# A two-layer encoder trunk: ScalarE and VectorE work behind later weight casts, PSUM banks by hand, operands loaded during P7

## The chip, the cores and the metric

The kernel runs on one core of one Trainium2 chip. The metric is the device time of one execution in microseconds (us), median of the runs shown. TensorE (PE) multiplies, VectorE (DVE) and ScalarE (ACT) work on elements, GpSimd (POOL) does a little of that and starts DMAs, and SyncE (SP) starts nearly all loads. Each engine works through its own instructions in the order in which they stand.

## What is computed

The reference runs two layers over 512 tokens of width 2048:

```
h = rmsnorm(x, g_pre)
z = h @ w_in                       # gq gk gv gg ga | aq ak av ag
log_a = log_sigmoid(ga @ w_alpha + b_alpha) / 16
o_gla = rmsnorm(gla_chunk_causal(gq, gk, gv, log_a), g_gla) * silu(gg)
o_att = rmsnorm(chunk_band_attention(aq, ak, av, rel_bias), g_att) * silu(ag)
y = concatenate([o_gla, o_att]) @ w_out
return x + rmsnorm(y, g_post)
```

The input projection has 14 column blocks of 512, the output projection four. The first blocks to be computed are the gates (AG, GG) and the attention values (AV).

## The kernel before

**A pair of blocks as seven products.** Two column blocks are computed together by `Pair` (L383). The matrix product is cut into halves of rows, of the inner dimension and of columns, and computed with seven products, P1 to P7, where eight would be plain. Each product runs over four chunks c = 0 to 3; one chunk of one product is a *job*, 12 matmuls of 128x512 in the front pairs (L480). A product's left operand is a block of activations or a sum of such blocks (S1 for P5, S2 for P6, S4 for P3, S3 for P7, and A22 for P4; P1 and P2 use plain blocks a11c and a12c). Its right operand is a weight block or a sum of weight blocks: `H` holds the running sum, `raw` a freshly loaded block. Numbers are kept in two parts to hold float32 precision: `wh` is the rounded weight, cast by ScalarE (L235), and `wl` the rest, subtracted by VectorE (L240). Weight sums for P5, P6 and P4 are made by VectorE at L224. So a job needs, in this order: a DMA from `in_w_dram` (L170, on SP's queue), perhaps a weight sum (L224), a cast on ScalarE (1.05 us), a subtraction on VectorE (1.22 us), then its matmuls.

**What is prepared ahead.** All jobs stand in one list, `stream`. After the matmuls of each job, `ahead` (L281) issues the load for up to five jobs on, the cast for up to four on and the low part for up to three on. There are four buffers each of `raw`, `H`, `wh` and of the operands `sa`, and three of `wl`. Program order on each engine is thus the order in which the Python code issues, as far as the scheduler, which works with its own cost model, does not move an instruction ahead; `tc.issue_after(x)` makes an instruction stand behind x.

**The front pairs.** Each layer begins with three pairs, (AG0, AG1), (GG0, GG1) and (AV0, AV1). A *head* runs P1 and P2 of the three in the order P1 of the first, P1 of the second, P2 of the first, P2 of the second, P1 of the third, P2 of the third (`HEAD`). Meanwhile the activations are scaled and split: in layer 0, `prep_chunk` scales a chunk (L690 on ScalarE, L688 on VectorE), casts it (L113) and subtracts (L114), which gives the operand a11c or a12c in use a little later. Then the rest of each pair runs in turn: P5, a mix of P6 and P3, P7, P4. The second and third pair ("second" in the code) load H again at P5, and with it the S1 operand from DRAM (L214, into the slots g8, g11, g14 and g15), where the first pair takes its S1 from SBUF.

**The banks.** The sums stand in PSUM: two banks X and two banks Y of the pool `ps_mm`, which has four in rotation. X takes P1 and P2, then P6, P7; Y takes P5 and P3. ScalarE copies p1 (L408) and later puts it back as X's first value (L415, in `open`); after P7 it copies X to Y (L503), on which P4 adds. P4's result in Y leaves through silu on ScalarE (L834) for the gates, or through a scaled copy (L944) for the values. The banks of the next pair are handed out in rotation, so that P5 of the next pair fills the two banks that P4 of the pair before has just filled.

**Side steps.** Scaling of activations, token squares (L535), sums, norms and the forget gate are Python generators in a list `tasks`; `pump` runs the next step of the first one some times after each job. They are issued in between, on the same engines. At the end of the second front pair, ScalarE loads another table of functions (L61), and VectorE scales the forget gate's input (L872).

Of the kernel before, what the change touches and what calls it, by code (L numbers as in the profile page):

```python
# [35 lines left out]
def hybrid_trunk(  # L36
# [19 lines left out]
    ps_mm = ctx.enter_context(tc.tile_pool(name="ps_mm", bufs=4, space=PSUM))  # L56
# [104 lines left out]
    lows = []  # L161
    rows = {}

    class Job:
# [8 lines left out]
        def load(self):  # L173
# [42 lines left out]
        def high(self):  # L216
# [17 lines left out]
            with tc.issue_after(last_evac[0]) if last_evac[0] else nullcontext():  # L234
                last_cast[0] = nc.scalar.copy(self.wh, src).ins  # L235

# [11 lines left out]
    stream = []  # L248
    for l in range(L):
        infos = [{"early": True, "direct": True}, {"early": True, "second": True}, {"early": True, "second": True}]  # L250
        for k, i in HEAD:
# [12 lines left out]
    done = {"load": 0, "high": 0, "low": 0}  # L264
# [7 lines left out]
    def take(l, blk, kind, c):  # L272
# [3 lines left out]
        for what in ("load", "high", "low"):  # L276
            prepare(what, i + 1)
# [62 lines left out]
    def std_gemm(l, blk, outs, chunks, operand, evac, rate=0.0, skip=0, lag=0, strict=False):  # L340
        pss = {o: ps_mm.tile([P, W], F32, tag="mm", name=nm("mm")) for o in outs}
# [35 lines left out]
    def pair_banks():  # L377
        return [ps_mm.tile([P, W], F32, tag="mm", name=nm("mm")) for _ in range(2)]
# [4 lines left out]
    class Pair:  # L383
        def __init__(self, l, pair, consume, feature_major=False, early=False, end=False, scaled=True, seeded=False, keep=ev):
# [3 lines left out]
            self.banks = {"X": pair_banks, "Y": pair_banks, "Z": aux_banks}  # L388
# [22 lines left out]
        def open(self, *names):  # L411
            for name in names:
                self.acc[name] = self.banks[name]()
            for t in range(2):
                nc.scalar.copy(self.acc["X"][t], self.keep["p1"][t])  # L415
# [71 lines left out]
        def run(self, prods, rate=0.0, skip=0, after=None):  # L487
            pace = Pace(rate, skip)
            for k, c in prods:
# [3 lines left out]
                if c == self.last:  # L493
                    if k == "P1":
                        self.copies("p1", self.acc["X"])
                    elif k == "P5":
                        self.copies("p5", self.acc["Y"])
                    elif k == "P6":
                        self.copies("x", self.acc["X"])
                    else:  # L500
                        if k == "P7" and self.seeded:
                            for t in range(2):
                                nc.scalar.copy(self.acc["Y"][t], self.acc["X"][t])  # L503
                        for t in range(2):
                            self.finished(k, t)
                        if k == "P7" and self.early and not self.seeded:
                            self.copies("x", self.acc["X"])
                if after is not None:
                    after(k, c)
                pace()  # L510

# [315 lines left out]
    def layer(l):  # L827
# [113 lines left out]
        def av_consume(j, h, t, src, comb):  # L941
# [16 lines left out]
            Pair(l, FRONT[1], gate_consume(0), scaled=False, **how),  # L958
            Pair(l, FRONT[2], av_consume, keep=early_kept, **how),
        ]  # L960
        for n, (k, i) in enumerate(HEAD):
# [5 lines left out]
        front[0].open("Y", "X")  # L967
        front[0].run(early_rest(C_IN), rate=1.0)
        drain()
        tasks.append(forget_gate())  # L970
        front[1].open("X", "Y")
        front[1].run(early_rest(C_IN), rate=0.25)
# [5 lines left out]
        front[2].open("Y", "X")  # L978
        front[2].run(early_rest(C_IN))
        S_on.clear()  # L980
# [175 lines left out]
        fast_gemm(l, PAIRS[0], qk_consume(0), rate=2.1, feature_major=True, scaled=False)  # L1156
        fast_gemm(l, PAIRS[1], qk_consume(1), rate=2.1, feature_major=True, scaled=False)
# [37 lines left out]
        fast_gemm(l, PAIRS[2], kq_consume, rate=2.1)  # L1195
# [171 lines left out]
        fast_gemm(l, PAIRS[3], gv_consume, rate=4, after=fetch_operands)  # L1367
# [93 lines left out]
        fast_gemm(l, W23, w_consume, rate=1.5, end=True, after=fetch_last, scaled=False)  # L1461
# [13 lines left out]
        std_gemm(l, NB_IN + 1, (2, 3), OO, operand_out, last_evac, rate=1.5, lag=3 if last else 2, strict=last)  # L1475
# [63 lines left out]
```

## Time and profile before

| quantity | value |
| --- | --- |
| runs | 1633.35, 1633.65 and 1630.3 us |
| median | 1633.35 us |
| the profiled execution's own time | 1632.18 us |
| its span in the profile | 1630.4 us |
| its mean granted TensorE clock | 0.992 |
| TensorE busy | 1602.3 us, 8818 matmuls |
| VectorE busy | 1258.3 us |
| ScalarE busy | 923.8 us |
| DMA, mean | 287 GB/s |

How to read the profile: times in rows are us from the start of the span. A row of the timeline has the start, the duration, the engine, the line of the kernel, the operation, what it writes and reads, and in square brackets how long the engine stood idle before it and what released it. "PEclk" is the clock that TensorE was granted, as a share of the full one. DMA share is the mean busy share of the core's 16 DMA engines. A busy TensorE may be at half its pace, so the count of matmuls in a stretch tells more than its busy time.

### The profile page before, as it was taken

To read this page: it belongs to the slowest core of one execution; us is meant where nothing else is said; L and a number is where in the kernel's file an instruction comes from. 1 tells how busy PE (TensorE), PEld (TensorE's weight loads), DVE (VectorE), ACT (ScalarE), POOL (GpSimd) and SP (SyncE) were. 2 spreads that over 40 slices of the span, in tenths; PEclk is the share of its full clock that TensorE was granted. 3 is DMA by queue.
4 is the path that set the end of the run, shared out by engine and by line. 5 is a ranking of instruction groups with operands and counts; after the bars stand their busy time and mean duration, and the time that the engine had idled before them with its cause. 6 is when DMAs were issued, how large, how long until landed. Compare 5 with 4: busy or idle time off the path is not lost.

```text
span 1630.4 us, 24529 instructions
## 1 busy us (share of the span) xinstructions
PE 1602.3 (98%) x8818; PEld 1359.0 (83%) x8818; DVE 1258.3 (77%) x1580; ACT 923.8 (57%) x1534; POOL 177.4 (11%) x302
## 2 busy tenths in 40 slices
PE   9999999999999999999999999999999999999997
PEld 6777879999988887788787877899999888777886
DVE  6778788786877866678878877877868778766887
ACT  8465554456676545554685545444566865445543
POOL 1121000000101001310121100000011011013100
PEclk9999999999999999999999999999999999999999
DMA  9959777867868689799968788678588686978986
GB/s 371 375 195 401 269 253 258 295 222 250 297 223 292 223 317 324 277 364 329 344 235 328 261 329 300 229 250 313 176 292 302 213 285 222 357 251 327 383 314 233
DMA packets 150618, 467.84 MB, mean 287 GB/s; under 512 B 16492, under 2 KB 35956, under 8 KB 150496
## 3 DMA queue, kind: packets, MB, share of 16 engines
q1 hardware_dynamic: 127232, 385.79, 67.0%
q0 software_dynamic: 22688, 79.53, 12.8%
q8 instruction: 70, 1.15, 0.3%
q10 hardware_dynamic: 576, 0.95, 0.2%
q14 instruction: 52, 0.43, 0.1%
HBM read 393.01 MB, written 72.11 MB: 285 GB/s over the span
## 4 chain that ended last, share of the span: by engine, by line
PE 89%; DMA 5%; DVE 2%; ACT 2%; issue 1%; SPq 0%; DVEq 0%; POOLq 0%; ACTq 0%
PE mm L480 49%; PE mm L467 20%; PE mm L360 10%; DMA raw<-in_w_dram 2%; PE ax L1051 2%; DMA H<-in_w_dram 2%; DVE wl L240 1%; PE ax L480 1%; PE ax L1034 1%; PE ax L1251 1%; PE ax L1217 1%; ACT wh L235 1%; PE ax L1013 1%; PE ax L1014 1%; DMA t<-r 1%
## 5 line engine op out<-in xcount | busy, mean ns | idle before, releaser
L240 DVE TENSOR_TENSOR wl<-raw,wh 128x1024 fp32r<-128x1024 f32 x256 | 312.0, 1221 | 123.3 <-PE mm L480 35.9
L235 ACT CAST wh<-raw 128x1024 fp32r<-128x1024 f32 x256 | 269.0, 1052 | 229.5 <-PE mm L480 96.1
L235 ACT CAST wh<-H 128x1024 fp32r<-128x1024 f32 x239 | 250.9, 1052 | 227.3 <-PE mm L480 90.6
L240 DVE TENSOR_TENSOR wl<-H,wh 128x1024 fp32r<-128x1024 f32 (+1 forms) x241 | 292.6, 1216 | 102.1 <-PE mm L480 46.3
L480 PE MATMUL mm<-wh,sa 128*128 128x512 f32 x1088 | 345.2, 392 | 0.0
L480 PE MATMUL mm<-wh,g 128*128 128x512 f32 x832 | 266.3, 399 | 9.3 <-ACT wh L235 6.0
L480 PEld LDWEIGHTS mm<-wh,sa 128*128 128x128 f32 x1088 | 203.2, 188 | 43.0 <-issue 1.5
L467 PE MATMUL mm<-sa,wh 128*128 128x256 f32 x1280 | 236.3, 285 | 0.0
L480 PE MATMUL mm<-wh,a 128*128 128x512 f32 x704 | 229.6, 397 | 2.1 <-ACT a L113 1.0
L480 PE MATMUL mm<-wl,sa 128*128 128x512 f32 x544 | 212.7, 391 | 0.0
L224 DVE TENSOR_TENSOR H<-H,raw 128x1024 f32<-128x1024 f32 x160 | 194.2, 1220 | 22.4 <-DMA H<-in_w_dram 14.3
L467 PEld LDWEIGHTS mm<-sa,wh 128*128 128x128 f32 x1280 | 199.4, 191 | 0.2
L480 PEld LDWEIGHTS mm<-wh,g 128*128 128x128 f32 x832 | 159.9, 193 | 46.3 <-ACT wh L235 8.3
L467 PE MATMUL mm<-sa,wl 128*128 128x256 f32 x640 | 180.7, 283 | 0.0
L480 PE MATMUL mm<-wl,g 128*128 128x512 f32 x416 | 165.9, 399 | 3.8 <-DVE wl L240 3.7
L480 PEld LDWEIGHTS mm<-wh,a 128*128 128x128 f32 x704 | 131.7, 188 | 35.4 <-issue 3.7
L480 PE MATMUL mm<-wl,a 128*128 128x512 f32 x352 | 138.4, 395 | 1.3 <-DVE wl L240 1.3
L467 PEld LDWEIGHTS mm<-sa,wl 128*128 128x128 f32 x640 | 122.3, 191 | 0.2
L480 PEld LDWEIGHTS mm<-wl,sa 128*128 128x128 f32 x544 | 102.2, 188 | 21.8 <-DVE wl L240 0.8
L480 PEld LDWEIGHTS mm<-wl,g 128*128 128x128 f32 x416 | 80.2, 193 | 23.3 <-DVE wl L240 6.4
L467 PE MATMUL mm<-a,wh 128*128 128x256 f32 x512 | 94.3, 285 | 0.0
L523 POOL TENSOR_TENSOR sm<-sm,cst 128x4 f32<-128x4 f32 (+2 forms) x40 | 49.3, 1233 | 325.3 <-DVE sm L1411 134.2
(208 smaller groups left out, 2269.9 us busy)
## 6 DMA issues: line engine op xcount, KB each, us to landing
raw<-in_w_dram SPq DMA_DIRECT2D x352, 512.0 KB, 5.5
sa<-S SPq DMA_DIRECT2D x128, 512.0 KB, 4.8
H<-in_w_dram SPq DMA_DIRECT2D x63, 512.0 KB, 5.7
S<-g POOLq DMA_DIRECT2D x32, 512.0 KB, 6.2
g<-S SPq DMA_DIRECT2D x32, 512.0 KB, 6.6
sa<-A SPq DMA_DIRECT2D x32, 512.0 KB, 6.0
oS<-g POOLq DMA_DIRECT2D x32, 512.0 KB, 6.4
sa<-oS SPq DMA_DIRECT2D x32, 512.0 KB, 5.1
```

The costliest lines, as they stand in the source:

```text
L224: nc.vector.tensor_tensor(out=h, in0=h, in1=r, op=ALU.add)
L235: last_cast[0] = nc.scalar.copy(self.wh, src).ins
L240: last_low[0] = nc.vector.tensor_tensor(out=self.wl[:, kk, :], in0=self.src[:, kk, :], in1=self.wh[:, kk, :].bitcast(F32), op=ALU.subtract ...
L360: mm = nc.tensor.matmul(pss[o], a[:, part, t], rhs[:, kk, :], start=(i == 0 and kk == 0 and m == 0), stop=(i == n - 1 and kk == 1 and m == 2),
L467: nc.tensor.matmul(dst, lhs[:, kk, f], a[:, part, tok], start=(fresh and kk == 0 and m == 0 and ft % 2 == 0), stop=(c == self.last and kk ...
L480: nc.tensor.matmul(out_ps[t], a[:, part, tok], rhs[:, kk, :], start=(fresh and kk == 0 and m == 0), stop=(c == self.last and kk == 1 and m ...
L523: return nc.gpsimd.tensor_tensor(out=out_r, in0=v, in1=mhalf[:, : v.shape[-1]], op=ALU.pow).ins
L1013: nc.tensor.matmul(ps[:, :n], self.qh[:, t], self.kl[:, :n], start=False, stop=False)
L1014: nc.tensor.matmul(ps[:, :n], self.ql[:, t], self.kh[:, :n], start=False, stop=True)
L1034: nc.tensor.transpose(ps[:, j * P : (j + 1) * P], self.prob[i][:, j * P : (j + 1) * P], ident)
L1051: nc.tensor.matmul(o, self.pt[i][:, j * P : (j + 1) * P], av[hd // 4, j // 2][:, j % 2, (hd % 4) * P : (hd % 4 + 1) * P], start=(j == 0), ...
L1217: mm = nc.tensor.matmul(self.ps_u[cc][:, tt * 256 : (tt + 1) * 256], kd[p][r, tt, hk], self.gv[p][r, tt, hv], start=True, stop=True,).ins
```

## The change

Four things are changed, all in the front pairs but the second and a part of the third.

1. `behind()` is new. While the front pairs run, the evictions at a product's end (now in `close`), the first values of X in `open`, and every side step that `pump` issues stand behind the last but one cast on ScalarE and the last but one low part on VectorE that have been issued.
2. `ps_mm` has one buffer for each of four tags, and `bank(i)` names them. Each pair says where its X lies (`x_bank` 0 or 2); Y lies in the two other banks. The front pairs have X in 0, 2, 0, so that P5 of the next pair fills the banks that P7 of the pair before leaves.
3. The operand loads (S1 to S4, A22) are taken out of `load` into `bring`, which `ahead` calls for four jobs ahead where `load` did it for five; `bring_next` loads the next front pair's S1 of chunk c behind the job P7 c of the pair that runs.
4. In layer 0 the norms of the second token half take turns with the token sums, where they stood ahead of them.

```
     @contextmanager
     def behind():
         if in_front[0] and len(casts) > 1 and len(lows) > 1:
             with tc.issue_after(casts[-2]), tc.issue_after(lows[-2]):
                 yield
         else:
             yield
...
+        def bring(self):
+            k, c, p = self.kind, self.c, self.pair
+            end = self.b0 == W23[0]
             name = LEFT.get(k)
+            if self.a is not None:
+                return
...
-        for what, n in (("load", 3), ("high", 3), ("low", 3), ("load", 4), ("high", 4), ("load", 5)):
-            if what != "load" and all(z.kind == "std" for z in stream[i + n - 2 : i + n]):
+        for what, n in (("load", 3), ("high", 3), ("low", 3), ("load", 4), ("high", 4), ("load", 5), ("bring", 4)):
+            if what in ("high", "low") and all(z.kind == "std" for z in stream[i + n - 2 : i + n]):
...
-                    entry[1]()
+                    with behind():
+                        entry[1]()
...
-                    next(tasks[0])
+                    with behind():
+                        next(tasks[0])
...
-    def pair_banks():
-        return [ps_mm.tile([P, W], F32, tag="mm", name=nm("mm")) for _ in range(2)]
+    def bank(i):
+        return ps_mm.tile([P, W], F32, tag=f"mm{i}", name=nm("mm"))
+
+    def pair_banks(first):
+        return lambda: [bank(first), bank(first + 1)]
...
-            self.banks = {"X": pair_banks, "Y": pair_banks, "Z": aux_banks}
+            self.banks = {"X": pair_banks(x_bank), "Y": pair_banks(2 - x_bank), "Z": aux_banks}
...
+                    with behind():
+                        self.close(k)
...
-            Pair(l, FRONT[1], gate_consume(0), scaled=False, **how),
+            Pair(l, FRONT[1], gate_consume(0), scaled=False, x_bank=2, **how),
...
-            tasks.insert(0, first_norms(1))
+            tasks[0] = beside(tasks[0], first_norms(1), 2)
...
+        def bring_next(i):
+            def f(k, c):
+                if k == "P7":
+                    next(z for z in stream if z.pair is infos_of[l][i] and (z.kind, z.c) == ("P5", c)).bring()
+            return f
+
+        front[0].open(0)
+        front[0].run(early_rest(C_IN), rate=1.0, after=bring_next(1))
```

Line numbers above 216 differ between the two versions: the cast L235 is now L251, the evictions L408, L415, L503, L834 and L944 are now L432, L439, L534, L862 and L972, the squares L535 are now L563.

**The start of layer 0, ScalarE.** a110, a111 and a112 are the operands of the first three jobs, H_3, H_5, H_7 and H_9 the weights of the first four; before:

```order
L690 ACTIVATE g8_4_213<-g8_4_213,gcol_206 128x256
L113 CAST a110_17_257<-g8_4_213 128x512
L232 CAST wh_15_249<-H_3_212 128x512
L235 CAST wh_20_274<-H_5_218 128x1024
L690 ACTIVATE g11_6_220<-g11_6_220,gcol_206 128x256
L113 CAST a111_32_302<-g11_6_220 128x512
L235 CAST wh_21_276<-H_7_222 128x1024
L690 ACTIVATE g0_8_224<-g0_8_224,gcol_206 128x256
L113 CAST a112_33_307<-g0_8_224 128x512
L235 CAST wh_22_278<-H_9_226 128x1024
```

The same place in the changed kernel:

```order
L718 ACTIVATE g8_4_213<-g8_4_213,gcol_206 128x256
L113 CAST a110_17_257<-g8_4_213 128x512
L248 CAST wh_15_249<-H_3_212 128x512
L251 CAST wh_20_274<-H_5_218 128x1024
L251 CAST wh_21_276<-H_7_222 128x1024
L251 CAST wh_22_278<-H_9_226 128x1024
L718 ACTIVATE g11_6_220<-g11_6_220,gcol_206 128x256
L718 ACTIVATE g0_8_224<-g0_8_224,gcol_206 128x256
L113 CAST a111_32_302<-g11_6_220 128x512
L113 CAST a112_33_307<-g0_8_224 128x512
```

The casts of the third and fourth weight moved ahead of the second job's operand a111 and of a112.

**The end of the head in layer 0, ScalarE.** pc is the copy of P1 of the third pair from its banks mm_120 and mm_121, the lines with norm_1 are P2's eviction from the same banks, L535 squares of tokens, wh_143 and after the weights for P5 of the first pair; before:

```order
L235 CAST wh_116_764<-raw_114_746 128x1024
L408 COPY pc_140_862<-mm_120_776 128x512
L235 CAST wh_123_792<-raw_117_766 128x1024
L408 COPY pc_141_864<-mm_121_777 128x512
L235 CAST wh_126_810<-raw_124_794 128x1024
L235 CAST wh_131_832<-raw_127_812 128x1024
L235 CAST wh_138_858<-raw_132_834 128x1024
L944 ACTIVATE t2_154_942<-mm_120_776,norm_1_209 128x512
L944 ACTIVATE t2_155_945<-mm_121_777,norm_1_209 128x512
L535 ACTIVATE t2_164_973,sm_163_972<-g12_128_814 128x1024
L535 ACTIVATE t2_165_975,sm_163_972<-g13_129_815 128x1024
L235 CAST wh_143_881<-H_3_212 128x1024
```

In the changed kernel:

```order
L251 CAST wh_116_764<-raw_114_746 128x1024
L251 CAST wh_123_792<-raw_117_766 128x1024
L251 CAST wh_126_810<-raw_124_794 128x1024
L251 CAST wh_131_832<-raw_127_812 128x1024
L432 COPY pc_140_862<-mm_120_776 128x512
L432 COPY pc_141_864<-mm_121_777 128x512
L251 CAST wh_138_858<-raw_132_834 128x1024
L251 CAST wh_143_881<-H_3_212 128x1024
L251 CAST wh_146_900<-H_5_218 128x1024
L251 CAST wh_149_919<-H_7_222 128x1024
L972 ACTIVATE t2_154_942<-mm_120_776,norm_1_209 128x512
L972 ACTIVATE t2_155_945<-mm_121_777,norm_1_209 128x512
```

The copies of P1 moved behind three casts of P2's weights, P2's evictions behind three casts of P5's, and the squares to after that.

**The seam from the first to the second front pair in layer 0, SP.** S100 to S103 are the S1 operands of the second pair, the H its weights for P5; before:

```order
L170 DMA raw_221_1264<-in_w_dram 128x1024
L170 DMA raw_224_1284<-in_w_dram 128x1024
L170 DMA raw_227_1303<-in_w_dram 128x1024
L170 DMA raw_231_1325<-in_w_dram 128x1024
L214 DMA g8_232_1327<-S100_84 128x1024
L170 DMA raw_242_1365<-in_w_dram 128x1024
L214 DMA g11_243_1367<-S101_85 128x1024
L170 DMA H_230_1323<-in_w_dram 128x1024
L170 DMA raw_249_1393<-in_w_dram 128x1024
L214 DMA g14_250_1395<-S102_86 128x1024
L170 DMA H_241_1363<-in_w_dram 128x1024
L170 DMA H_248_1391<-in_w_dram 128x1024
```

In the changed kernel:

```order
L180 DMA raw_221_1266<-in_w_dram 128x1024
L230 DMA g8_222_1268<-S100_84 128x1024
L180 DMA raw_227_1292<-in_w_dram 128x1024
L230 DMA g11_228_1294<-S101_85 128x1024
L180 DMA raw_233_1318<-in_w_dram 128x1024
L230 DMA g14_234_1320<-S102_86 128x1024
L180 DMA raw_238_1341<-in_w_dram 128x1024
L230 DMA g15_243_1355<-S103_87 128x1024
L180 DMA raw_247_1376<-in_w_dram 128x1024
L180 DMA H_237_1339<-in_w_dram 128x1024
L180 DMA raw_251_1397<-in_w_dram 128x1024
L180 DMA H_246_1374<-in_w_dram 128x1024
```

The four S1 loads, of which three stood among the H loads and one behind them, now stand one by one among the raw loads ahead of every H.

More of the change, by code (lines that the diff above doesn't have):

```diff
@@ L1 @@
-from contextlib import ExitStack, nullcontext
+from contextlib import ExitStack, contextmanager, nullcontext
 from itertools import product
@@ L160, in hybrid_trunk, with behind @@
     made = set()
-    lows = []
+    lows, casts = [], []
+    in_front = [False]
+    @contextmanager
+    def behind():
+        if in_front[0] and len(casts) > 1 and len(lows) > 1:
+            with tc.issue_after(casts[-2]), tc.issue_after(lows[-2]):
+                yield
+        else:
+            yield
     rows = {}
@@ L235, in high @@
                 last_cast[0] = nc.scalar.copy(self.wh, src).ins
+            casts.append(last_cast[0])
         def low(self):
@@ L262, in hybrid_trunk @@
         stream += [Job(l, "std", c, NB_IN + 1) for c in OO]
-    done = {"load": 0, "high": 0, "low": 0}
+    done = {"load": 0, "bring": 0, "high": 0, "low": 0}
     cursor = [0]
@@ L275, in take @@
         assert (job.l, job.b0, job.kind, job.c) == (l, blk, kind, c)
-        for what in ("load", "high", "low"):
+        for what in ("load", "bring", "high", "low"):
             prepare(what, i + 1)
@@ L338, in __call__, with std_gemm @@
             self.due -= int(self.due)
-    def std_gemm(l, blk, outs, chunks, operand, evac, rate=0.0, skip=0, lag=0, strict=False):
-        pss = {o: ps_mm.tile([P, W], F32, tag="mm", name=nm("mm")) for o in outs}
+    def std_gemm(l, blk, outs, chunks, operand, evac, rate=0.0, skip=0, lag=0, strict=False, banks=range(4)):
+        pss = {o: bank(b) for o, b in zip(outs, banks)}
         pace = Pace(rate, skip)
@@ L383, in hybrid_trunk, with __init__ @@
     class Pair:
-        def __init__(self, l, pair, consume, feature_major=False, early=False, end=False, scaled=True, seeded=False, keep=ev):
+        def __init__(self, l, pair, consume, feature_major=False, early=False, end=False, scaled=True, seeded=False, keep=ev,
+                     x_bank=0):
             self.l, self.b0, self.consume = l, pair[0], consume
@@ L409, in copies, with open @@
                 self.keep[name].append(e)
[L411 to L415, printed above, removed]
+        def open(self, x_bank):
+            self.acc = {"X": pair_banks(x_bank)(), "Y": pair_banks(2 - x_bank)()}
+            with behind():
+                for t in range(2):
+                    nc.scalar.copy(self.acc["X"][t], self.keep["p1"][t])
         def combine(self, ps, h, t, kept, sign, op):
@@ L493, in run @@
                 if c == self.last:
[L494 to L507, printed above, removed]
+                    with behind():
+                        self.close(k)
                 if after is not None:
@@ L510, in run, with close @@
                 pace()
+        def close(self, k):
+            if k == "P1":
+                self.copies("p1", self.acc["X"])
+            elif k == "P5":
+                self.copies("p5", self.acc["Y"])
+            elif k == "P6":
+                self.copies("x", self.acc["X"])
+            else:
+                if k == "P7" and self.seeded:
+                    for t in range(2):
+                        nc.scalar.copy(self.acc["Y"][t], self.acc["X"][t])
+                for t in range(2):
+                    self.finished(k, t)
+                if k == "P7" and self.early and not self.seeded:
+                    self.copies("x", self.acc["X"])
     def fast_gemm(l, pair, consume, rate=0.0, after=None, end=False, **how):
@@ L1364, in gv_consume @@
                 tasks.append(heads if j else beside(heads, early_sums(), 3))
-        fast_gemm(l, PAIRS[3], gv_consume, rate=4, after=fetch_operands)
+        fast_gemm(l, PAIRS[3], gv_consume, rate=4, after=fetch_operands, x_bank=2)
         A.clear()
@@ L1459, in fetch_last @@
                 nc.sync.dma_start(flat(op_att[1, i]), oa_d[l][1, i])
-        fast_gemm(l, W23, w_consume, rate=1.5, end=True, after=fetch_last, scaled=False)
+        fast_gemm(l, W23, w_consume, rate=1.5, end=True, after=fetch_last, scaled=False, x_bank=2)
         for c in range(4):
@@ L1473, in last_evac @@
                 pass
-        std_gemm(l, NB_IN + 1, (2, 3), OO, operand_out, last_evac, rate=1.5, lag=3 if last else 2, strict=last)
+        std_gemm(l, NB_IN + 1, (2, 3), OO, operand_out, last_evac, rate=1.5, lag=3 if last else 2, strict=last, banks=(2, 3))
         drain()
```

21 lines of the change are left out of this document (11 added, 10 removed).

## The prediction

> **What bounds the kernel now.** I read the page first, for the engine that is always at work, then the windows of TensorE over stretches of the front pairs, then its waits, and then the timelines of ScalarE and VectorE at the places that the waits name.
>
> ```profile
> PE 1602.3 (98%) x8818; PEld 1359.0 (83%) x8818; DVE 1258.3 (77%) x1580; ACT 923.8 (57%) x1534; POOL 177.4 (11%) x302
> ```
>
> TensorE (PE) is busy for 98% of the span, so the matmuls bound the kernel. Nothing in the change removes a matmul. It can only win where TensorE runs slower than its own pace, and that is a matter of a few stretches:
>
> ```profile
> core 0: us, PE busy (x), PEclk, DMA share, GB/s
> 162.00:186.00 24.00, 24.00 (x108) 1.00 0.61 202
> 62.00:78.00 16.00, 14.68 (x60) 1.00 1.03 393
> 86.00:100.00 14.00, 10.37 (x32) 0.76 0.61 202
> 146.00:156.00 10.00, 8.52 (x34) 1.00 1.03 413
> 207.00:219.00 12.00, 10.43 (x38) 0.86 1.02 378
> 950.00:962.00 12.00, 8.91 (x27) 0.72 0.92 348
> 1012.00:1024.00 12.00, 9.05 (x33) 0.86 1.02 359
> ```
>
> The first row is an undisturbed stretch: 108 matmuls in 24.00 us, 0.222 us each. What a stretch loses is its length less its matmuls at that pace. At 62 to 78 us that is 16.00 - 60 x 0.222 = 2.7 us; at 86 to 100, 14.00 - 32 x 0.222 = 6.9; at 146 to 156, 2.4; at 207 to 219, 3.6; at 950 to 962, 6.0; at 1012 to 1024, 4.7. The loss is larger than the idle time that the busy column leaves, because the granted clock sinks to 0.72 to 0.86 around the gaps. In layer 0 the places are P1 to P2 of the third pair (62 us), the end of the six head products (86), and the seams from the first pair to the second (146) and from the second to the third (207); in layer 1 the two seams again (950 and 1012). The last five lose 6.9 + 2.4 + 3.6 + 6.0 + 4.7 = 23.6 us.
>
> ```profile
> PE mm L480 <- ACT wh L235: 6.5, 5, 3.8
> PE mm L480 <- DVE wl L240: 4.9, 7, 1.7
> PE mm L480 <- ACT t L834: 3.1, 1, 3.1
> ```
>
> These are TensorE's waits (us, times, longest): for the casts of weights, for the low parts of weights, and once, 3.1 us long, for an eviction (L834, the silu of P4 of the pair before, whose banks P5 of the next pair is to fill).
>
> **Why the casts and low parts come late.** ScalarE (ACT) at the end of the head, then VectorE and ScalarE around the second seam, then ScalarE at the first seam of layer 1:
>
> ```profile
> 85.17 1.37 ACT L944 ACTIVATE t<-mm,norm 128x512 f32<-128x512 f32 x2 [7.80 <-PE mm L480]
> 86.43 1.04 ACT L535 ACTIVATE t<-g 128x1024 bf16<-128x1024 f32 x1
> ...
> 88.51 1.98 ACT L235 CAST wh<-H 128x1024 fp32r<-128x1024 f32 x2
> ```
>
> ```profile
> 208.05 1.23 DVE L224 TENSOR_TENSOR H<-H,raw 128x1024 f32<-128x1024 f32 x1 [0.39 <-DMA H<-in_w_dram]
> 209.19 0.68 DVE L872 TENSOR_TENSOR g<-ax,t 96x512 f32<-96x512 f32 x1
> 209.79 2.35 DVE L240 TENSOR_TENSOR wl<-H,wh 128x1024 fp32r<-128x1024 f32 x2
> ```
>
> ```profile
> 206.77 1.28 ACT L61 ACT_TABLE_LOAD   x1
> ```
>
> ```profile
> 951.84 1.04 ACT L235 CAST wh<-H 128x1024 fp32r<-128x1024 f32 x1 [7.49 <-DVE H L224]
> 952.79 1.26 ACT L834 ACTIVATE t<-mm,norm 128x512 f32<-128x512 f32 x2
> ```
>
> At 85 us ScalarE had sat idle for 7.80 us behind an eviction that waited for the last matmul of a product, with casts of resident weights queued behind it; then came two squares of 1.04 us, and the cast only at 88.51. At 951.84 it is the other way round: the cast waited for a weight sum, and the eviction that frees the banks stood behind it.
>
> **The change part by part.** *Evictions and side steps behind later casts.* Nothing is added or removed; the casts of the next three jobs go first. At the end of the head the new order has the three casts ahead of L944 (now L972), so the cast of 88.51 can be done in the 7.80 us that were idle. All 6.9 us go, the half-clock part with them.
>
> *Banks by hand.* P5 of the next pair now gets the banks that P7 drained, so the 3.1 us wait for L834 goes, and P4's evictions have four products' time. What would be late next there is the weight sum.
>
> *The first sums during P7.* The seams wait for H, the weight block that P5 needs:
>
> ```profile
> H<-in_w_dram SPq DMA_DIRECT2D x4, 512.0 KB, 11.3
> raw<-in_w_dram SPq DMA_DIRECT2D x6, 512.0 KB, 5.9
> H<-in_w_dram SPq DMA_DIRECT2D x63, 512.0 KB, 5.7
> 114.00:132.00 18.00, 1.00 0.86 308
> ```
>
> The first is the DMA view at the first seam of layer 0 (132 to 148 us): 11.3 us to landing, against 5.7 over the kernel (third row). The second is the same queue during P6 to P7, 5.9. At the seam the queue carries four H, the raw blocks and four S1, at 413 GB/s (row 146 to 156), so an S1 of 512 KB costs 0.524 MB / 413 = 1.27 us and four cost 5.1. On SP's queue these four now stand ahead of the seam's H, so the last H comes up to 5.1 us earlier. That nearly covers its lateness of 11.3 - 5.7 = 5.6. The cover is the spare rate during P7: at share 0.86 over 18 us there are 18 x 0.14 = 2.5 us of it in sight (last row), so between 2.5 and 5.1. I take the seams as cured, 2.4 + 3.6 + 6.0 + 4.7 = 16.7, since the table load, L872 and the P4 evictions also step behind the casts there; the other end is half of it. Together with 6.9 that makes 23.6.
>
> *P1 to P2 of the third pair.*
>
> ```profile
> 72.22 0.59 ACT L408 COPY pc<-mm 128x512 f32<-128x512 f32 x1 [6.33 <-PE mm L480]
> 72.70 1.05 ACT L235 CAST wh<-raw 128x1024 fp32r<-128x1024 f32 x1
> ```
>
> The copy held the cast back for 6.33 us; now three casts go ahead of it. But P2 adds into the bank that this copy reads, and the third cast waits for a load while the queues run at share 1.03. So P2 may wait for the copy where it waited for the cast. Between -1.5 (copy after a cast and a half more) and all of the 2.7 I take a gain of 1.0.
>
> *The start of layer 0 pays.* The operand a111 of the second job is itself a side step (scale, cast, subtraction). ScalarE did it after the second weight's cast; it now stands behind the fourth's (H_9), on SP's queue the last of the first four weights.
>
> ```profile
> 4.73 0.71 SPq L170 DMA_DIRECT2D H<-in_w_dram  x1
> ```
>
> ```profile
> DMA to landing us min/median/max: 3.1/6.1/7.4
> ```
>
> ```profile
> 9.16 0.50 ACT L690 ACTIVATE g<-g,gcol 128x256 f32<-128x256 f32 x1
> 9.69 0.62 ACT L113 CAST a<-g 128x512 fp32r<-128x512 f32 x1
> ...
> 12.22 1.05 ACT L235 CAST wh<-H 128x1024 fp32r<-128x1024 f32 x1
> ```
>
> ```profile
> 8.93 0.39 PE L480 MATMUL mm<-wh,a 128*128 128x512 f32 x1
> 10.36 0.50 PE L480 MATMUL mm<-wh,a 128*128 128x512 f32 x1 [1.03 <-ACT a L113]
> 25.23 0.50 PE L480 MATMUL mm<-wl,a 128*128 128x512 f32 x1 [0.50 <-DVE wl L240]
> ```
>
> Issued at 4.73, that weight lands 7.4 us later, at 12.1, and no order on ScalarE can cast it sooner: 12.2 + 1.05 + two scales of 0.50 + the cast of 0.62, less overlaps of about 0.1 at each step, is 14.7. TensorE's second job so starts at 14.7 in place of 10.36: 4.3 us. The gap of 9.3 to 14.7 is 5.4 us long. Gaps of 3.8 and 3.1 us went with clocks of 0.76 over 14.00 us and 0.72 over 12.00, which is 14.00 x 0.24 = 12.00 x 0.28 = 3.4 us each; I add 3.4. The wait of 0.50 at 25.23 is absorbed. The start costs 4.3 + 3.4 - 0.5 = 7.2; bounds 0 (if the later jobs, whose operands then stand ready, have waits to give back) and 7.7.
>
> [...]
>
> *Evictions that come later.*
>
> ```profile
> 90.39 0.63 ACT L535 ACTIVATE t<-bias 128x512 bf16<-128x512 f32 x1
> 135.65 0.57 ACT L503 COPY mm<-mm 128x512 f32<-128x512 f32 x1 [1.21 <-PE mm L480]
> 136.13 1.05 ACT L235 CAST wh<-H 128x1024 fp32r<-128x1024 f32 x1
> ```
>
> Four squares of 0.63 us (first row; 2.5 us together) now stand ahead of the copies of the first P5; P3 needs the bank one job of 12 x 0.222 = 2.7 us later, so the most is 2.5, and I take 0.8. The seeds from P7 to P4 (last two rows: the first seed, then a cast) now stand behind that cast, 1.05 us, and both P4 and its first matmul wait for them. Of 0 to 2 us I take 0.4 at each of the two first pairs: 0.8.
>
> *The sum.* 23.6 + 1.0 - 7.2 - 0.8 - 0.8 = 15.8 us less. The other reorderings, and the norms of the second half beside the token sums, hide under a TensorE that does not wait there; if that cover is gone I allow 1.5 either way. The profiled execution took 1632.18 us (span 1630.4), 1.17 below the median of 1633.35 and inside the runs of 1630.3 to 1633.65, so I sum against it: 1632.2 - 15.8 = 1616.4, forecast **1616**.
>
> **The rivals.** *The start costs less.* TensorE's later waits at the start absorb the delay, or the clock does not sink. For it: weights arrive early once the start is over; against it: only 0.50 us of wait was seen at 25.23. Without the clock's part 1613.0, without any cost 1616.4 - 7.2 = 1609. Chance 0.14.
>
> *H is late all the same.* The bytes are the same and spare rate in P7 covers only 2.5 of 5.1 us, so half of the 16.7 us stays: 1616.4 + 8.4 = 1625. For it: share 1.02 to 1.03 in three of the four seam rows; against it: the 3.1 us wait for L834 and the table load need no bytes. Chance 0.20.
>
> *Slower: evictions behind casts that wait for late weights.* The place is the seam of P7 to P4, in all six front pairs. The seeds stand behind the cast of the third P4 job; where its load is late by the 5.6 us above, the seeds come late, P4 waits, and the clock sinks. At the 3.6 us that the seam of 207 to 219 lost, six cost 21.6, less 0.8 counted: 1616.4 + 20.8 = 1637. It turns the gain into a loss from (15.8 + 0.8) / 6 = 2.8 us a seam. For it: a cast waited 7.49 us for its weight at 951.84; against it: during P6 and P7 loads land in 5.9 us. Chance 0.06. [...]
>
> *No net change.* What goes at one engine is waited for at another, 1632. The printed order does move, so I give it 0.05.
>
> **How the numbers follow.** The forecast case has 0.55. With the first two rivals 0.89 are faster by over 0.2% (3.3 us, about what a measurement of this kernel can tell from no change), 0.05 within it, 0.06 slower. The range goes from 1609 less the 1.5 and some of the 1.7 us at P1 to P2, 1605, to 1625 plus 1.5, 1626; outside lie the slower case, the unchanged one and the edges, under 0.2.
>
> **What would show it.** Right: TensorE's second job starts at 14 to 15 us with a wait for the operand; no idle time over 1 us at 86 to 100, and none for an eviction at the seams; H lands in 6 to 8 us there. Wrong: waits for casts or low parts at the seams with H still over 10 us, waits for the seeds (L534) or copies (L432) of more than 1 us at P4, P2 or P3, or a second job that starts by 11 us.

## The result and the profile after

The changed kernel took 1616.54 us (median of 4 runs, 1616.15 to 1618.52), the kernel before 1631.82 (4 runs, 1629.63 to 1633.65). The ratio is 0.9909, with a 95% interval of 0.9892 to 0.9927: 15 us less, as the forecast of 1616 had it. The profiled execution of the changed kernel is the longest of its four, 1618.52 us with a span of 1616.7, so the two profiles lie 13.7 us apart.

TensorE's waits after the change (us, times, longest):

```profile
PE mm L504 <- DVE wl L257: 7.9, 7, 2.0
PE mm L504 <- ACT a L113: 5.2, 1, 5.2
PE mm L504 <- ACT mm L534: 2.0, 2, 1.5
```

The waits for casts of whole blocks (6.5 us before) and for P4's eviction (3.1) are gone. In their place stand the operand a111 at the start, the seeds of P4 (L534, the copies from X to Y on which P4 adds), and more waits for low parts than before (4.9). Of the 7.9 us for low parts 6.9 are at the seams. The windows show where (length, TensorE busy with its matmuls, granted clock, DMA share, GB/s):

```profile
14.00:20.00 6.00, 4.46 (x14) 0.72 1.04 406
62.00:78.00 16.00, 16.00 (x72) 1.00 1.01 390
84.00:98.00 14.00, 14.00 (x63) 1.00 0.63 209
128.00:138.00 10.00, 8.00 (x35) 1.00 1.03 413
140.00:152.00 12.00, 10.27 (x45) 1.00 0.97 381
940.00:952.00 12.00, 9.95 (x44) 1.00 1.02 390
998.00:1012.00 14.00, 12.20 (x48) 0.88 0.96 335
```

Rows two and three are full: P1 to P2 of the third pair and the end of the head lose nothing any more. The other rows are the start, the seeds of P4 in the first pair, and three of the four seams.

To see where the 13.7 us came from, I set the time of each matmul in one trace against that of the matmul with the same number in the other (both have 8818). The changed kernel is behind by 5.2 us at the second job's first matmul, by 6.5 at 16 us of the kernel before, and by only 2.9 at 67 us. From there on it changes in steps:

| place | forecast, us | read from the two traces, us |
| --- | --- | --- |
| start, up to 67 us | +7.2 | +6.5 at first, +2.9 in the end |
| P1 to P2, third pair | -1.0 | -1.6 |
| end of the head | -6.9 | -7.3 |
| evictions of P5 and seeds of P4, layer 0 | +1.6 with layer 1 | +2.6 |
| first and second seam, layer 0 | -2.4, -3.6 | -1.5, -1.9 |
| between the layers | 0, within 1.5 | -1.9 |
| layer 1 up to its first seam | in the seeds above | +0.3 |
| first and second seam, layer 1 | -6.0, -4.7 | -4.0, -1.2 |
| sum | -15.8 | -13.7 |

The 1.9 us between the layers come mainly from 812 to 817 us of the kernel before, where TensorE waited three times for the weights of the last product of layer 0 (0.53, 0.60 and 0.53 us); after the change it does not wait there.

So the number was right and two of its larger terms were not: the seams gave 8.6 us of the 16.7, and the start cost 2.9 of the 7.2. The experiments went after these two, after the seeds, and after what each part of the change is worth.

### The profile page after: what moved, and what is told of

It is laid out like the page before. It is cut to its first block, busy times and chain, and to the rows that moved or that the text cites. A ratio compares the mean times of both kernels' runs of the same rounds, so it can differ in the third digit from the quotient of the medians.

```text
span 1616.7 us, 24522 instructions
## 1 busy us (share of the span) xinstructions
PE 1590.8 (98%) x8818; PEld 1355.4 (84%) x8818; DVE 1257.7 (78%) x1580; ACT 923.4 (57%) x1534; POOL 181.5 (11%) x302
## 4 chain that ended last, share of the span: by engine, by line
PE 92%; DMA 4%; DVE 2%; issue 1%; ACT 1%; SPq 0%; DVEq 0%; POOLq 0%; ACTq 0%
PE mm L504 49%; PE mm L491 20%; PE mm L380 11%; DMA H<-in_w_dram 3%; PE ax L1087 2%; PE ax L504 1%; DMA raw<-in_w_dram 1%; PE ax L1070 1%; PE ax L1253 1%; PE ax L1287 1%; DVE wl L257 1%; PE ax L1049 1%; PE ax L1050 1%; PE ax L686 1%; PE ax L1048 1%
## 5 line engine op out<-in xcount | busy, mean ns | idle before, releaser
L251 ACT CAST wh<-raw 128x1024 fp32r<-128x1024 f32 x256 | 269.4, 1053 | 237.9 <-PE mm L504 111.5
L251 ACT CAST wh<-H 128x1024 fp32r<-128x1024 f32 x239 | 251.0, 1052 | 230.1 <-PE mm L504 88.0
L504 PE MATMUL mm<-wh,g 128*128 128x512 f32 x832 | 259.2, 391 | 0.0
```

The source lines that it names most:

```text
L504: nc.tensor.matmul(out_ps[t], a[:, part, tok], rhs[:, kk, :], start=(fresh and kk == 0 and m == 0), stop=(c == self.last and kk == 1 and m ...
```

## The parts of the change, undone one by one

All times below are medians; each run stood beside runs of the kernel before on the same chip, whose medians were 1631.2 to 1633.9. The runs were spread over several chips, so where two of them differ by less than about 3 us the medians alone do not decide, and the waits in the traces have to carry the argument.

**no_behind.** Nothing is queued behind the casts:

```
-        if in_front[0] and len(casts) > 1 and len(lows) > 1:
+        if False:
```

> The changed kernel with nothing queued behind the casts; banks by hand, S1 during P7 and the norms beside the token sums stay. If the traces compared by matmul give the parts (head end 7.3 us and P1 to P2 of the third pair 1.6 lost again; start 2.9 and seeds before P4 3.2 won back), it takes 1616.5 + 8.9 - 6.1 = about 1619. If the order on ScalarE also did the work at the seams, 1624 or more. If banks and loads did nearly all, under 1617.

Measured: 1623.54 us (1620.21 to 1627.49), ratio to before 0.9943 (0.9925 to 0.9961). That is 7.0 above the changed kernel; the profiled execution, 1621.06, was near the lower end. Its waits are those of the kernel before again, in which ScalarE stood idle for 7.80 us (until 85.17 us) with an eviction at the head of its queue and the casts of resident weights behind it:

```profile
PE mm L504 <- ACT wh L251: 8.2, 6, 4.8
PE mm L504 <- DVE wl L257: 5.9, 8, 2.0
```

Matmul by matmul it loses 7.9 us at the end of the head and 1.6 at P1 to P2, and wins back 3.5 at the start and 2.6 at layer 0's first P4, much as the first reading had it. At the four seams it loses only 0.4 us together, so the order on ScalarE did little there. This one execution is only 2.5 us longer than the profiled one of the changed kernel. By the medians the order on ScalarE is worth about 7 us, and banks and loads together the other 8 to 9.

**old_banks.** P5 fills the banks of P4 again, with everything else as changed:

```
-        front[1].open(2)
+        front[1].open(0)
```

> The changed kernel, but the second front pair's rest takes its banks the other way round, so that P5 fills the banks in which P4 of the pair before has just ended, at both seams of a layer. Theory one (the banks by hand are what makes evictions behind casts affordable): P5 waits at every seam for an eviction that stands behind casts of late H, 3 to 6 us at each of four, 1628 to 1640. Theory two (in the kernel before only one of four seams waited for it, 3.1 us): 1618 to 1621.

Measured: 1634.82 us (1632.65 to 1639.27), ratio 1.0028 (1.0017 to 1.0038): slower than the kernel before. The first row of its waits:

```profile
PE mm L504 <- ACT t L862: 18.0, 4, 5.7
```

All four seams wait for P4's eviction, 18.0 us together, where the kernel before waited once, 3.1. The eviction stands behind casts of H, and the casts wait for the sums that H goes into (2.69 us for the one ahead of the eviction at 147.83 us). So the banks are what makes the new order affordable; the one without the other is a loss.

**no_bring.** S1 is loaded four jobs ahead by `ahead`, and not during P7:

```
-        front[0].run(early_rest(C_IN), rate=1.0, after=bring_next(1))
+        front[0].run(early_rest(C_IN), rate=1.0)
```

> The changed kernel without the S1 loads during P7: S1 is loaded four jobs ahead, among the H loads. Theory one (the seams wait for H behind the S1 bytes, 1.27 us each, four at a seam): H lands up to 5.1 us later and the four seams lose together 6 to 12 us more, 1623 to 1628. Theory two (the loads are at full rate before and after, so moving bytes moves the backlog only, and the seams were helped by the banks and the order on ScalarE): within 2 us of 1616.5.

Measured: 1620.87 us (1618.19 to 1621.57), ratio 0.9923 (0.9909 to 0.9938), 4.3 above the changed kernel. The matmuls say less: the four seams change by +1.0, +1.2, +1.8 and -1.3 us, so they lose 2.7 together. That is between the two theories: the early S1 does help, by less than the 6 to 12 us that I had set on it.

## Why the seams gave only half

The DMA view of the first seam of layer 0 (132 to 148 us before, 128 to 144 after) has four H each; the last number is the median of us from issue to landing. It was 11.3 before, and after the change:

```profile
raw<-in_w_dram SPq DMA_DIRECT2D x5, 512.0 KB, 8.7
H<-in_w_dram SPq DMA_DIRECT2D x4, 512.0 KB, 9.1
```

So H got 2.2 us faster, not the 5.1 that the sum assumed, and the raw blocks beside it now take 8.7. Two causes were possible: bytes ahead of H in the queue, or a late issue. For the second, VectorE (low parts that free an H buffer) and SP's issues after the change, first VectorE, then SP:

```profile
129.06 1.20 DVE L257 TENSOR_TENSOR wl<-H,wh 128x1024 fp32r<-128x1024 f32 x1
...
131.32 1.21 DVE L257 TENSOR_TENSOR wl<-H,wh 128x1024 fp32r<-128x1024 f32 x1
...
133.93 1.22 DVE L257 TENSOR_TENSOR wl<-H,wh 128x1024 fp32r<-128x1024 f32 x1
```

```profile
130.29 0.33 SPq L180 DMA_DIRECT2D H<-in_w_dram  x1
131.42 0.33 SPq L180 DMA_DIRECT2D raw<-in_w_dram  x1
132.56 0.33 SPq L180 DMA_DIRECT2D H<-in_w_dram  x1
134.04 0.33 SPq L180 DMA_DIRECT2D raw<-in_w_dram  x1
135.17 3.98 SPq L180 DMA_DIRECT2D H<-in_w_dram  x2
```

P4's low parts end at 130.26, 132.53 and 135.15, and H is issued at 130.29, 132.56 and 135.17: the four H buffers are all in use by P4, and each load starts the moment that P4 gives one back. I had not read this in the trace before, where it stands too: the first H of this seam is issued at 134.45 us, 0.03 us after a low part ends. Four runs on the two causes:

**few_bytes.** P5 of the second and third pair leaves out its second weight block and adds H to itself:

```
+                if p.get("second"):
+                    p["r", c] = p["H", c]
```

> The changed kernel, but in the second and third front pairs P5 adds H to itself in place of a freshly loaded block, so 16 loads of 512 KB, four at each of the four seams, are left out of the computation. Theory one (the seams' rest of about 8 us is the queue's backlog): no wait for a low part over 0.5 us is left at the seams and it takes 1608 to 1610. Theory two (H is late because its buffer comes free late): the waits stay, 1615 to 1617.

Measured: 1617.04 us (1616.26 to 1618.18), ratio 0.9901 (0.9886 to 0.9916), no change, and 6.0 us of waits for low parts. From 125 to 150 us the queues carried 8.59 MB in place of 9.74, and H still took 8.9 us at the first seam. It speaks against a plain count of bytes, but not as clearly as planned, since raw loads still stood between the H on SP's queue (at 131.14 and 133.41 us):

```profile
H<-in_w_dram SPq DMA_DIRECT2D x4, 512.0 KB, 8.9
```

**h5a.** A fifth H buffer, with the scratch rings t2 and ev cut from 8 to 7 and from 6 to 5:

```
-                    p["H", c] = self.fetch(rtile("H"), b0, top)
+                    p["H", c] = self.fetch(rtile("H", bufs=5), b0, top)
```

> The changed kernel with five H buffers in place of four (one buffer less each of two other scratch rings pays for the room). In the trace after, each of the four H loads of a seam is issued within 0.05 us of the end of the low part (L257) that frees its buffer. Theory one (the buffers hold H back): H lands 2 to 3 us earlier and the seams win 4 to 8 us, 1609 to 1613. Theory two (the queue's backlog decides, 9 us from issue to landing at full rate): less than 2 us. A loss would be the scratch rings' doing.

Measured: 1630.66 us (1627.47 to 1632.6), ratio 0.998 (0.997 to 0.999). Slower, but by the matmuls the seams won (2.0, 1.9, 2.1 and 3.6 us) and no wait for a low part was left at them; some 23 us were lost elsewhere, above all among the attention heads (486 to 508 us and 1108 to 1310 us), where the smaller rings are used. A run that mixes two causes, so it was made again without the second:

**h_slots.** Two H blocks go into slots that are empty at that time:

```
+                    tag = {(GG0, 0): "g0", (AV0, 1): "g1"}.get((b0, c))
+                    p["H", c] = self.fetch(slot(tag, [2, 512]) if tag else rtile("H"), b0, top)
```

> The changed kernel with two more places for H and nothing taken from elsewhere: the second pair's first H and the third pair's second H go into two slots that lie empty between the sums and the values, so each H of a seam takes a buffer that was freed one job earlier. Theory one (the release of H's buffers by P4's low parts holds the seams back): the waits for low parts at the seams, 7.9 us in the trace after, go to under 2 us, as they went in the run with five buffers, without that run's losses among the heads: 1608 to 1611. Theory two (that run's seams gained from something else): 1615 to 1617.

Measured: 1611.81 us (1609.15 to 1612.51), ratio 0.9882 (0.9866 to 0.9899), 4.7 less than the changed kernel. Its waits:

```profile
PE mm L505 <- ACT a L113: 4.7, 1, 4.7
PE mm L505 <- ACT mm L535: 4.2, 2, 3.0
```

No wait for a low part appears among them. The seams won 2.0, 1.9, 2.5 and 3.7 us, 10 in all, so the buffers did hold the seams back, though H took no less time from issue to landing at the first (10.0 us): its first three loads were issued 0.9 to 1.8 us earlier. About 4 us were given back at the seeds of P4 in the first pairs (L535 here). The longer wait, 2.95 us at 133.53, is in layer 0: the cast ahead of the seeds waited 2.50 us for its weight sum, and after the gap TensorE's matmuls came 0.43 us apart until 138.4 us, in place of 0.23 ahead of it. Why that sum came late is not shown.

**bring_early.** S1 comes four jobs earlier still, with the buffers as they were:

```
-                if k == "P7":
+                early = (("P6", 2), ("P6", 3), ("P3", 2), ("P3", 3))
+                if (k, c) in early:
+                    c = early.index((k, c))
```

> The changed kernel with the next pair's S1 loaded four jobs earlier still, during the last four jobs of P6 and P3 in place of P7. Leaving the S1 loads of P7 out cost 4.3 us. Theory one (every S1 that leaves the stretch ahead of H brings H in earlier): 2 to 4 us less, 1612.5 to 1614.5. Theory two (what is loaded earlier only pushes back the raw blocks ahead of H, and H cannot be issued before P4's low parts have freed its buffers): within 1 us of 1616.5.

Measured: 1618.48 us (1616.78 to 1620.1), ratio 0.9909 (0.9894 to 0.9925), 1.9 more than the changed kernel. And yet the seams were cured:

```profile
H<-in_w_dram SPq DMA_DIRECT2D x4, 512.0 KB, 5.3
```

```profile
PE mm L504 <- ACT mm L534: 6.9, 2, 4.2
PE mm L504 <- ACT a L113: 5.2, 1, 5.2
PE mm L504 <- DVE wl L257: 0.8, 2, 0.6
```

With S1 out of P7, H lands in 5.3 us instead of 9.1 and the waits for low parts fall from 7.9 to 0.8 us, of which 0.2 are at a seam. The seams won 2.0, 1.7, 2.4 and 2.8 us, 8.9 in all, and 7.6 of it went at the first pairs' P4, where the seeds now wait 6.9 us. At the first seam of each layer that lateness of P4 itself gave H almost 4 us more time, so only the second seams (1.7 and 2.8 us, with H landing in 6.2 and 6.5 us instead of 9.2 and 9.6) speak for the queue alone. So neither cause alone is the answer: H is late because its buffer comes free late and because the queue ahead of it is full, and either an earlier issue or an emptier queue cures it. What decides whether the time is kept is the place of the seeds.

## The seeds of P4

At the first pair's P4 after the change, ScalarE and then TensorE:

```profile
131.50 1.05 ACT L251 CAST wh<-H 128x1024 fp32r<-128x1024 f32 x1 [2.56 <-DVE H L240]
132.45 1.06 ACT L534 COPY mm<-mm 128x512 f32<-128x512 f32 x2
```

```profile
131.16 0.39 PE L504 MATMUL mm<-wh,g 128*128 128x512 f32 x1
133.09 0.50 PE L504 MATMUL mm<-wh,sa 128*128 128x512 f32 x1 [1.54 <-ACT mm L534]
```

P7 was done at 131.6, ScalarE was free, but the cast in front waited for its weight sum until 131.50, so the seeds came at 132.45.

**free_seeds.** The two copies are made ahead of `close`, outside `behind`:

```
+                    if k == "P7" and self.seeded:
+                        for t in range(2):
+                            nc.scalar.copy(self.acc["Y"][t], self.acc["X"][t])
                     with behind():
                         self.close(k)
```

> The changed kernel, but the two seeds that copy X to Y between P7 and P4 are not queued behind the casts. The forecast priced their delay at 0.8 us in all; the trace after shows 2.0 us of waits for them and a loss of 2.6 us (layer 0) and 0.6 us (layer 1) at the first pair's P4. If these are all due to the seeds' place: 1613 to 1614. If a seed ahead of a cast makes the cast wait as before: within 1 us of 1616.5.

Measured: 1614.93 us (1614.21 to 1618.35), ratio 0.9896 (0.9878 to 0.9915). The gain of 1.6 is half of what the first theory said and within the spread of its runs. At layer 0's first P4 the edit did not do what it was made for. The scheduler still put a cast ahead of the two copies, that cast waited for its sum, and TensorE waited 1.55 us as before:

```profile
130.21 1.05 ACT L251 CAST wh<-H 128x1024 fp32r<-128x1024 f32 x1 [2.55 <-DVE H L240]
131.16 1.06 ACT L520 COPY mm<-mm 128x512 f32<-128x512 f32 x2
```

So alone it decides nothing about the seeds' place. In `best`, below, the copies do stand ahead of that cast, and no seed is waited for.

## The start

**no_start.** In layer 0 `behind` works from the second product on:

```
-        in_front[0] = True
         for n, (k, i) in enumerate(HEAD):
+            in_front[0] = l > 0 or n > 0
```

> The changed kernel, but in layer 0 evictions and side steps go behind the casts only after the first product. The forecast had the start cost 7.2 us with 0.5 given back later: then this kernel takes 1609 to 1610 us against 1616.5. The rival, read from the two traces by the time of the same matmul (5.6 us behind at the second job, 6.5 at 16 us, 2.6 at 38 us, 2.9 at 67 us), is that waits which the kernel before had at 28 to 45 us absorb most of it: then the gain is about 3 us, 1613 to 1614.

Measured: 1616.56 us (1615.32 to 1617.82), ratio 0.9899 (0.9883 to 0.9915): no gain at all. In its trace TensorE is 5.4 us ahead of the changed kernel at the second job, still 5.4 at 48 us, and 0.9 at 80 us. The place, ScalarE and then TensorE in no_start:

```profile
70.57 1.04 ACT L251 CAST wh<-raw 128x1024 fp32r<-128x1024 f32 x1 [1.27 <-DVE wl L257]
71.82 1.04 ACT L251 CAST wh<-raw 128x1024 fp32r<-128x1024 f32 x1 [0.21 <-DMA raw<-in_w_dram]
72.78 1.07 ACT L432 COPY pc<-mm 128x512 f32<-128x512 f32 x2
```

```profile
73.41 0.65 PE L504 MATMUL mm<-wh,a 128*128 128x512 f32 x1 [2.55 <-ACT pc L432]
```

The third pair's P2 adds into the banks that pc copies. The copy stands behind three casts. When TensorE ran out of work at 70.86 us, one of them was just under way and the last still had to wait for its load, so the copy came at 72.78. In the changed kernel TensorE came to P1's end 5.4 us later, all three casts were done before it (the last by 74.61 us, the copy came at 75.14), and there was no wait at all: the start's loss and this one are one and the same time, paid once.

**start_p1.** As no_start, with the copies of P1 behind nothing:

```
-                    with behind():
+                    with nullcontext() if k == "P1" else behind():
                         self.close(k)
```

> As no_start, and the copies of P1 are queued behind nothing either. In no_start the 5.9 us won at the start shrank to 0.9 by 80 us, most of it at the third pair's P2, which waited 2.55 us for the copy (L432) that stood behind a cast whose load was late. Theory one (the copy's place gives it back): the wait goes, 1613 to 1614. Theory two (the loads of the head are at full rate and set when P2's weights are there, whoever waits): the wait moves to a cast or a low part, within 1 us of the 1616.5 of no_start.

Measured: 1616.39 us (1614.09 to 1616.58), ratio 0.9893 (0.9878 to 0.9908). The wait for the copy went and a wait for a cast came (2.2 us in two pieces): now the copy, which waits for P1's end, blocks the casts behind it, as in the kernel before. By this run's time alone one would say that the loads set the pace, though the four casts then run back to back without waiting for one.

**best.** h_slots, free_seeds and start_p1 in one.

> h_slots, with the seeds before P4 and the copies of P1 queued behind nothing, and the first product of layer 0 as before. If the parts add up: 8 us from H, 1 to 2 from the seeds, 0 to 1 from the start, 1606 to 1609. If seeds ahead of a cast cost what they win once H is early: as h_slots.

Measured: 1605.93 us (1604.19 to 1606.75), ratio 0.9848 (0.9832 to 0.9864), 10.6 less than the changed kernel. The parts more than add up (4.7 + 1.6 + 0.2): the seams win what they won in h_slots, and the first P4 of layer 0, where h_slots lost 3.4 us, wins 2.6 (both against the changed kernel), since the seeds now stand ahead of the cast. P2 of the third pair still waits:

```profile
73.99 0.73 PE L505 MATMUL mm<-wh,a 128*128 128x512 f32 x2 [1.62 <-ACT wh L252]
75.25 0.50 PE L505 MATMUL mm<-wl,a 128*128 128x512 f32 x1 [0.53 <-DVE wl L258]
```

**p1_mid.** best, with the copies of P1 behind two of the three casts (`behind(n)` puts what it holds behind the n-th last cast and low part):

```
-                    with nullcontext() if k == "P1" else behind():
+                    with behind(3 if k == "P1" else 2):
                         self.close(k)
```

> best, but the copies of P1 stand behind one cast less than the other evictions, in place of behind none: with three casts ahead (no_start) P2 of the third pair waited 2.55 us for the copy, with none ahead (best) 1.62 us for a cast and 0.53 us for a low part. Theory one (only the copy's place gives the start's 5.4 us back): P2 starts without a wait over 0.5 us and the whole takes 1602 to 1604. Theory two (the loads of the head set when P2's weights are there): the wait moves to a cast or low part, within 1 us of the 1605.9 of best.

Measured: 1603.89 us (1603.62 to 1604.29), ratio 0.9831 (0.9808 to 0.9855). ScalarE and TensorE's windows there:

```profile
68.44 1.05 ACT L252 CAST wh<-raw 128x1024 fp32r<-128x1024 f32 x1 [1.58 <-DMA raw<-in_w_dram]
69.39 0.58 ACT L433 COPY pc<-mm 128x512 f32<-128x512 f32 x1
70.26 0.59 ACT L433 COPY pc<-mm 128x512 f32<-128x512 f32 x1 [0.29 <-PE mm L505]
70.75 1.05 ACT L252 CAST wh<-raw 128x1024 fp32r<-128x1024 f32 x1
```

```profile
56.00:68.00 12.00, 12.00 (x54) 1.00 1.02 412
68.00:80.00 12.00, 12.00 (x54) 1.00 1.01 395
```

The copy comes as P1 ends, the next cast right behind, and P2 starts without a wait, with the loads at full rate all the same (share 1.02 and 1.01). So it was the copy's place that gave the start's time back, not the loads. At 75 us p1_mid is 6.4 us ahead of best, 4.2 of it from P1 to P2; in these two profiles 3.8 are lost again by 149 us, at the head's end and in the first pair. The medians differ by 2.0, which is not clear of noise: the two runs were on different chips, and the intervals of their ratios overlap. The waits at P2 are what shows it. This is the fastest version that I ran, 12.6 us below the changed kernel.

## Why the prediction was right, and where its terms were not

- **The bound.** Right: TensorE is still busy for 98% of the span with the same 8818 matmuls, and all but 1.9 us of the gain came from the named stretches.
- **The end of the head.** Right, 7.3 us for 6.9; the run without the new order loses them again. After the change three casts stand done before the eviction, and the clock stays at 1.00.
- **P1 to P2.** Gained 1.6 for 1.0. The doubt in that step (P2 adds into the bank that the copy reads, and a cast ahead of the copy is late) was the mechanism that no_start showed; it stayed hidden in the changed kernel only because the start was late.
- **The start.** The step "The start costs 4.3 + 3.4 - 0.5 = 7.2" had the right event (second job at 15.5 us in the profile, forecast 14.7, and slow matmuls after it) and was mis-sized. Seven other runs with this start have the second job at 13.9 to 14.6 us; the profiled execution also waited 0.6 us for the cast of its first weight. The clock took 6.00 x 0.28 = 1.7 us here, not 3.4: it stood at 0.50 for 3.41 us, where it did so for 6.83 us in the two stretches of the kernel before from which the 3.4 was read (the last section). The term that failed is the 0.5: 6.5 - 2.9 = 3.6 us were given back by 67 us. In the medians the late start cost nothing that can be seen, since it would have been lost at P2.
- **The seams.** The step that failed is "I take the seams as cured, 2.4 + 3.6 + 6.0 + 4.7 = 16.7". They gave 8.6. I had priced the S1 bytes and taken H's place in SP's order for the time of its issue; the H buffers, which P4 gives back one job at a time, were not in the sum, and P7 was not the empty place that I took it for. At the first seam H landed 2.2 us sooner, not 5.1, and h_slots, with earlier issues alone, won the seams 10 us more. The rival "H is late all the same" had the size right (half stays), and its reason, bytes, as one of two.
- **The banks.** Right that the 3.1 us wait for the eviction goes, but it was never worth 3.1 us. TensorE's row in the kernel before is

```profile
953.53 1.37 PE L480 MATMUL mm<-wh,g 128*128 128x512 f32 x2 [3.09 <-ACT t L834]
```

  The cast that this matmul also needs ended at 951.84 + 1.04 = 952.88 us, so only the last 0.6 us were the eviction's; the rest was H's lateness, and 2.05 us of wait for a low part stand there now. Too little was said of the other side: without the banks the change would have been a loss of 3 to 6 us against the kernel before (old_banks). That is the slower rival's mechanism, evictions behind casts of late weights, at the seams in place of P7 to P4.
- **The seeds.** 0.8 forecast, 2.0 us of waits in two places, and about 2.6 us lost around layer 0's first P4 alone (of which a low part had 0.46); no_behind won the same 2.6 back. It is the same mechanism, below the 2.8 us a seam from which it would have decided.
- **Between the layers.** 1.9 us came from a place that I had covered with 1.5 either way, mainly three waits of the kernel before that are gone. What in the change took them away was not tried.

That the forecast stood to within 1 us is in part luck: the seams' 8.1 us too much and the start's 4.3 us too much are of opposite sign, with the layer boundary and the 1 to 2 us between profiled and median runs making up most of the rest.

## What to carry to other kernels

On an engine that both frees banks and prepares operands, and that stands idle behind a late eviction as ScalarE did here (7.80 us at the end of the head before the change), look for each eviction's place among the casts. Of the three places tried for the copies of P1 the best was behind the casts that can end before the product does, and ahead of the rest: behind two casts TensorE did not wait, behind none it waited 1.62 us for a cast and 0.53 for a low part, and behind three 2.55 us for the copy. Then check in the trace that the order came out as written; in free_seeds it did not. Before pricing a load by the bytes in front of it, look at what its issue waits for: here the issues followed a buffer's release within 0.03 us, one more place for H at each seam moved the first three issues of the first seam 0.9 to 1.8 us forward (h_slots), and an emptier queue brought the landing down from 9.2 to 6.2 us at the second seam of layer 0 (bring_early). And a loss that is seen at one place and missing from the total may only stand in for another that comes later, so undo it alone before you pay for a cure.

## What the runs showed of the hardware

What a gap cost in clock here did not follow from its length alone. These windows of the changed kernel are around the second job's start and around the second seam of layer 1 (length, TensorE busy with its matmuls, granted clock, DMA share, GB/s):

```profile
11.00:15.10 4.10, 0.00 (x0) 1.00 1.04 402
15.10:18.51 3.41, 2.97 (x7) 0.50 1.04 405
18.52:22.00 3.48, 3.48 (x16) 1.00 1.04 406
1001.56:1004.96 3.40, 1.60 (x8) 1.00 1.04 384
1004.97:1008.38 3.41, 3.41 (x10) 0.50 0.95 332
1008.39:1012.00 3.61, 3.61 (x18) 1.00 0.82 287
```

In the clock records of the two profiles, before and after, the changes of one trace lie whole multiples of 3.413 us apart (in the changed kernel at 15.10, 18.52, 1004.97 and 1008.38 us). But for the program's last microseconds each stretch at 0.50 lasts 3.41 us or, in the kernel before from 89.13 to 95.95 and from 952.70 to 959.52 us, 6.83. In such a stretch the matmuls came 0.43 us apart (at 16.13, 16.56 and 16.99 us), at 1.00 0.22 to 0.23. At that pace it costs about half its length, so 1.7 or 3.4 us: that is where the 3.4 of the prediction and the 1.7 here come from. Two seams of layer 1 show that the length of the gap did not decide:

```profile
947.12 0.50 PE L504 MATMUL mm<-wl,g 128*128 128x512 f32 x1 [2.05 <-DVE wl L257]
```

```profile
1004.11 0.50 PE L504 MATMUL mm<-wl,g 128*128 128x512 f32 x1 [1.80 <-DVE wl L257]
```

After 2.05 us of wait the clock was 1.00 over the stretch, after 1.80 us it was 0.88 (the windows from 940 and from 998 us above): 14.00 x 0.12 = 1.7 us lost after the shorter gap and none after the longer. Counted in steps of 3.413 us from 15.10 us, the shorter gap lies within one step and the longer across two, with 1.87 us in the first of them. What decides is not shown.
